# The seam between two layers, block by block: a trunk of one SSD layer and one dilated-attention layer, with the keys' matmul order, the adaLN dot products and GpSimd's residual moved

## The chip, the cores and the metric

The kernel runs on one core of a Trainium2 chip. The metric is the device time of one launch in microseconds. A core has engines that work side by side and wait for each other through semaphores: TensorE (PE in the profile; its weight loads are PEld), VectorE (DVE), ScalarE (ACT), GpSimd (POOL), and SyncE (SP), whose queue issues all DMA transfers of this kernel in program order.

## What is computed

256 tokens of width 2048 pass through two layers. Each layer computes x <- LayerNorm(alpha*x + (1+gate)*mixer(x*(1+scale)+shift)), where shift, scale and gate come from a second input c (adaLN). Cut to what matters here:

```python
def _adaln(c, w, b):
    mod = silu(c) @ w + b
    shift, scale, gate = split(mod, 3, axis=-1)
...
def reference(x, c, ada_w, ada_b, ln_g, ln_b, ..., a_out_w, kv_w, b_in_w, b_out_w):
    for layer in range(2):
        shift, scale, gate = _adaln(c, ada_w[layer], ada_b[layer])
        h = x * (1.0 + scale) + shift
        if layer == 0:
            y = _ssd_mixer(h, ..., a_out_w)        # y @ a_out_w at its end
        else:
            y = _dilated_mixer(h, k_sh, v_sh, b_in_w, b_out_w)
        x = _layer_norm(alpha * x + (1.0 + gate) * y, ln_g[layer], ln_b[layer])
        if layer == 0:
            k_sh, v_sh = _shared_kv(x, kv_w)       # split(x @ kv_w, 2), 3 groups x 8 heads x 128
    return x
```

The shared keys and values use the normalised x itself; the queries use h of the second layer. All arithmetic is float32.

## The kernel before

**Products.** A float32 matrix product is made of three products of rounded parts: weight high by activation high, low by high, and high by low. Each weight piece (512 KB, [128, 1024]) is loaded to `raw`; ScalarE rounds it to `whi` (L93) and VectorE subtracts to get `wlo` (L95). There are six `raw` buffers and four of `whi` and `wlo`, so loads run some pieces ahead of TensorE. Three forms of the product occur:

- `tm_chunk` / `tm_mults` (L172 to L174): tokens on the partitions of the result, 512 weight columns streamed; for each k-tile and each of the two blocks of 128 tokens three matmuls of 512 columns. With `split_end`, the last pieces of the chunk are held and run for block 0 first and then for block 1.
- `cm_piece` / `cm_quads` (L119 to L121): weight columns on the partitions, 256 tokens streamed; three matmuls of 256 columns for each k-tile and block of 128 weight columns.
- `cm_wide` (L151, L152): the same layout, but the activations' high and low parts lie side by side in `xp`, so one matmul of 512 columns covers high by both parts (L151) and one of 256 columns adds low by high (L152). For each k-tile the order is: 512 and 256 for the first block of columns, then 512 and 256 for the second. The eviction adds the two halves (L156 ScalarE, L157 VectorE).

**Order.** The kernel is written as one program; each engine runs its instructions in the order in which they were written, unless `issue_after` pins an instruction behind another. The order of the work around the change is this. Layer 0: projections and the scan, with the eight groups g of the scan; the output product `wout`, four chunks n of 512 columns with 32 k-tiles each. After chunk n, `residual` adds the gated result to x (L650, L651, on VectorE) and takes statistics (L652). Then `ln_scale` makes mean and reciprocal deviation for both blocks together with small operations (L659 to L664), and `u` is normalised, block 0 on ScalarE (L687) and block 1 on VectorE (L689). The function `x_tiles` transposes `u` in 128x128 tiles on TensorE (L702) and applies the norm's gain and offset per partition: `xhi` by ScalarE (L705), `xtmp` and `xlo` by VectorE (L706, L707). The tiles are made two k-tiles ahead of the products that use them.

The first products of layer 1 are the keys of the first half of the heads (`hq` 0), all three groups at once in six PSUM tiles with `cm_quads`; then the keys of the second half with `cm_wide` and all values with `tm_chunk`. After that x is scaled and shifted in place to h (L750, L196). `queries(0)` then runs 24 pieces of `wbin` through `cm_wide`, three groups of two column halves of four pieces each; the attention of those heads follows it, then the same for the second half, the gate and the output product. The attention bias `bs` (L766) is loaded at the start of the queries.

**adaLN dot products.** The modulation of a layer is 48 columns of 128 outputs. Each is one load of 1 MB (`araw`, L230) and one VectorE operation with accumulation (`dot`, L237). They are put in a list of jobs, and `background(n, every)` is called once after each weight piece: it adds n to a counter, and each time the counter reaches `every` one job is done. `queue` prepares them: two loads are always out. `pin` holds a VectorE instruction before which no dot may be placed. Rates before: 1 in 3 in the output chunks n = 1 to 3 (16 columns queued), 4 in 9 in the keys of `hq` 1 and the values (32 columns, 72 pieces). The counter also runs on while no job waits.

**GpSimd.** Once the transposes have read `u`, it is multiplied by the norm's gain row and its offset row is added (L759, L760), because the last residual needs x in this form. GpSimd does it for each quarter n of 512 columns and both blocks. The rows are broadcast loads of 256 KB (`lnr`, L63), in two tiles with two buffers each.

Of the kernel before, what the change touches and what calls it, by code (L numbers as in the profile page):

```python
# [9 lines left out]
F32 = mybir.dt.float32  # L10
# [39 lines left out]
def trunk(ctx, tc, xT, x, c, par, cst, bias, lnrow, ada, wdt, win, wout, wkv, wk1, wbin, wbout, out):  # L50
# [39 lines left out]
    def split(raw, into=None, after=None):  # L90

        hi, lo = into or [wp.tile([P, 1024], F32R, name=n, bufs=4) for n in ("whi", "wlo")]
        S.activation(hi, raw, AF.Copy)  # L93
        with tc.issue_after(after) if after is not None else ExitStack():
            latest[0] = V.tensor_tensor(lo, raw, hi.bitcast(F32), op=ALU.subtract)  # L95
        return hi.rearrange("p (k n) -> p k n", k=2), lo.rearrange("p (k n) -> p k n", k=2)

    jobs, latest, pin = [], [None], [None]

    def background(n, every=1):  # L100

        state[0] += n
# [19 lines left out]

    def cm_quads(work, ahi, alo, pre=None, after=None):
        for q in range(KT // 2):
            if pre:
                pre(q)
            for src, ps in work:
                cm_piece(src, q, ps, ahi, alo, after=after if q == 0 else None)
# [11 lines left out]
    def cm_wide(src, dst, rate=(0, 1)):  # L140
# [3 lines left out]
        for q in range(KT // 4):  # L144
            hi, lo = (t.rearrange("p k n -> p (k n)").rearrange("p (k n) -> p k n", k=4)
                      for t in split(load_piece(src[q])))
            for k in range(4):
                kt = 4 * q + k
                for n in range(2):
                    c_ = slice(n * P, n * P + P)  # L150
                    T.matmul(ps[n], hi[:, k, c_], xp[:, kt], start=kt == 0, stop=False, skip_group_check=True)  # L151
                    T.matmul(ps[n][:, 0, :], lo[:, k, c_], xhi[:, kt, :], start=False, stop=kt == KT - 1,  # L152
# [46 lines left out]
    sm.tile([P, 8], F32, name="pad", bufs=1)  # L199
# [72 lines left out]

    with ExitStack() as cA:
        pa = cA.enter_context(tc.tile_pool(name="pa", bufs=1))

        y = [pa.tile([P, 2, 512], F32, name=f"y{g}") for g in range(G)]
# [11 lines left out]
        with ExitStack() as cS:  # L288
# [305 lines left out]
            for g in range(G - 1):  # L594
                if g == 1:
                    pin[0] = latest[0].ins
# [57 lines left out]
        def ln_scale(blocks=(0, 1)):  # L654
# [3 lines left out]
            for i, b in enumerate(blocks):  # L658
# [9 lines left out]
                [(1, "gate", kt) for kt in range(KT)]  # L668
        for n in range(4):
            ps = tm_chunk(wout[n], lambda kt: yhi[kt // 16][:, kt % 16, :], lambda kt: ylo[kt // 4][:, kt % 4, :],  # L670
                          nk=2 * KT, rate=(1, 3) if n else (0, 1), pre=None if n else y_ahead,
                          split_end=2 if n == 3 else 0)
            if n == 0:
                queue(pn, cols1[:16])
# [6 lines left out]
        drain()  # L681
        r, nb, nb_last = ln_scale()
        for c0_, c1_ in ((0, 256), (256, 512), (512, 1024), (1024, 1536), (1536, 2048)):
            for b in range(2):
                cs_ = slice(c0_, c1_)
                if b == 0:
                    S.activation(u[b][:, cs_], u[b][:, cs_], AF.Identity, bias=nb[:, b:b + 1], scale=r[:, b:b + 1])  # L687
                else:
                    V.tensor_scalar(u[b][:, cs_], u[b][:, cs_], r[:, b:b + 1], nb[:, b:b + 1],  # L689
                                    op0=ALU.mult, op1=ALU.add)  # L690
# [7 lines left out]
    def x_tiles(q):  # L698
        for kt in (2 * q, 2 * q + 1):
            pt = aux.tile([P, 512], F32, name="aux")[:, :L]  # L700
            for b in range(2):
                T.transpose(pt[:, b * P:b * P + P], u[b][:, kt * P:kt * P + P], ident)  # L702
            t = pl.tile([P, L], F32, name="xtmp")
            g_, b_ = pv("lng")[:, kt:kt + 1], pv("lnb")[:, kt:kt + 1]
            S.activation(xhi[:, kt, :], pt, AF.Identity, bias=b_, scale=g_)  # L705
            V.tensor_scalar(t, pt, g_, b_, op0=ALU.mult, op1=ALU.add)  # L706
            V.tensor_tensor(xlo[:, kt, :], t, xhi[:, kt, :].bitcast(F32), op=ALU.subtract)  # L707

    def ahead(q):

        if q == 0:
            x_tiles(0)
        if q < KT // 2 - 1:
            x_tiles(q + 1)

    kk = [pb.tile([P, 12, L], F32, name=f"kk{i}").rearrange("p (g i) l -> p g i l", g=NG) for i in range(2)]
    vt = [pb.tile([P, NG, 2, 512], F32, name=f"vt{i}") for i in range(2)]

    def evict_k(hq, g, ps):
        for w in range(2):  # L720
            S.activation(kk[hq][:, g, 2 * w:2 * w + 2, :], ps[w], AF.Copy)

    with ExitStack() as cL:
        pl = cL.enter_context(tc.tile_pool(name="pl", bufs=3))
        ex = cL.enter_context(tc.tile_pool(name="ex1", bufs=2, space=PSUM))
        ps = [acc_pair(), acc_pair(), acc_pair(ex)]
        cm_quads([(wkv[2 * g], ps[g]) for g in range(NG)], xhi, xlo, pre=ahead, after=nb_last.ins)
        for g in range(NG):
            evict_k(0, g, ps[g])

        R = (4, 9)
        pin[0] = latest[0].ins
        with tc.issue_after(nb_last.ins):
            queue(pl, cols1[16:])
            jobs.append(lambda: gate_out(1))
            for g in range(NG):
                for w in range(2):
                    cm_wide(wk1[2 * g + w], kk[1][:, g, 2 * w:2 * w + 2, :], rate=R)
            for hq in range(2):
                for g in range(NG):  # L740
                    ps = tm_chunk(wkv[6 + 2 * g + hq], hx, lx, rate=R)
                    for b in range(2):
                        S.activation(vt[hq][:, g, b, :], ps[b], AF.Copy)
            drain()

# [6 lines left out]

        for n in range(4):
# [206 lines left out]
```

## Time and profile before

| | us |
|---|---|
| median of 3 runs | 1300.86 |
| lowest and highest | 1299.53, 1302.91 |
| the profiled execution | 1303.79 |
| its span | 1302.0 |
| its mean granted TensorE clock | 0.988 of full speed |

The profile comes from one execution. A page of it gives, for the whole span, the busy time of each engine, the chain of work that ended last, and groups of instructions by source line. Other views used here are the timeline (start, duration, engine, line, operation, output and inputs; in brackets how long the engine was idle before it and what ended that), windows (busy time of each engine in a stretch, the granted clock, the DMA engines' busy share and GB/s), and the waits of an engine. Matmuls are pipelined, so the duration of one is longer than the distance to the next; prices of matmuls are read from start to start. A few per cent of the matmul records can be missing.

### The profile page before, as it was taken

The page shows a single profiled execution, that of the slowest core. Times are in us where ns is not written, and L with a number is a line of the kernel's source. Part 1 is how long each engine was busy: PE and PEld are TensorE (multiplying, and loading weights), DVE is VectorE, ACT ScalarE, POOL GpSimd, SP SyncE. Part 2 cuts the span into 40 slices and gives each one's busy share as a digit, 9 for nine tenths or more (in the row PEclk, how much of TensorE's full clock was granted, in tenths as well). Part 3 has the DMA queues.
Part 4 walks back from the last instruction along what each step waited for, and adds up shares of the span by engine and source line. Part 5 has one row for each costly group of instructions (what it writes and reads, how often), then busy time and mean ns, then how long its engine had stood idle before and what let it go on. Part 6 is the DMA issues. An engine that isn't in the chain of part 4 may idle for free.

```text
span 1302.0 us, 19326 instructions
## 1 busy us (share of the span) xinstructions
PE 1244.2 (96%) x7378; PEld 1096.7 (84%) x7378; DVE 1028.6 (79%) x1457; ACT 709.6 (55%) x1036; POOL 26.6 (2%) x20
## 2 busy tenths in 40 slices
PE   4999999999999999999999799999999999999995
PEld 3878988899898999878888699888887888888884
DVE  6689887899998778899775577988777757758677
ACT  3544457867587686864333444444435645444651
POOL 0000000000000000000000043000000000000000
PEclk9999999999999999999999899999999999999998
DMA  9999967696884556389977575999897864353561
GB/s 381 421 367 419 382 205 249 221 345 243 288 312 152 187 180 209 117 324 331 383 262 218 190 244 163 354 376 367 329 344 268 274 192 146 106 189 95 162 259 65
DMA packets 80445, 335.86 MB, mean 258 GB/s; under 512 B 8960, under 2 KB 9056, under 8 KB 67552
## 3 DMA queue, kind: packets, MB, share of 16 engines
q1 hardware_dynamic: 80352, 334.62, 71.7%
q8 instruction: 58, 0.95, 0.3%
q14 instruction: 35, 0.29, 0.1%
HBM read 332.41 MB, written 2.18 MB: 257 GB/s over the span
## 4 chain that ended last, share of the span: by engine, by line
PE 82%; DVE 9%; DMA 4%; ACT 3%; issue 2%; SPq 0%; DVEq 0%; ACTq 0%
PE acc L151 13%; PE acc L173 12%; PE acc L174 11%; PE acc L172 11%; PE acc L121 8%; PE acc L120 8%; PE acc L119 8%; PE acc L152 6%; DMA araw<-in_ada 4%; DVE araw L237 2%; DVE wlo L95 2%; PE py L579 1%; PE aux L788 1%; ACT whi L93 1%; DVE cacc L306 1%
## 5 line engine op out<-in xcount | busy, mean ns | idle before, releaser
L95 DVE TENSOR_TENSOR wlo<-raw,whi 128x1024 fp32r<-128x1024 f32 x395 | 484.9, 1240 | 191.4 <-ACT whi L93 189.9
L93 ACT ACTIVATE whi<-raw 128x1024 fp32r<-128x1024 f32 x395 | 412.8, 1056 | 334.8 <-PE acc L174 140.8
L119 PE MATMUL acc<-actT,whi 128*128 128x256 f32 x960 | 274.1, 288 | 23.4 <-ACT whi L93 19.3
L173 PE MATMUL acc<-wlo,actT 128*128 128x512 f32 x704 | 277.2, 394 | 3.2 <-DVE wlo L95 3.1
L121 PE MATMUL acc<-actT,wlo 128*128 128x256 f32 x960 | 272.3, 288 | 4.5 <-DVE wlo L95 4.4
L120 PE MATMUL acc<-actT,whi 128*128 128x256 f32 x960 | 273.8, 286 | 0.6 <-DVE actT L384 0.6
L172 PE MATMUL acc<-whi,actT 128*128 128x512 f32 x704 | 272.9, 395 | 0.8 <-ACT actT L634 0.7
L151 PE MATMUL acc<-actT,whi 128*128 128x512 f32 x704 | 250.9, 398 | 0.0
L237 DVE SCALAR_TENSOR_TENSOR araw<-araw,cb__72 128x2048 f32<-128x2048 f32 x96 | 219.4, 2286 | 17.0 <-DMA araw<-in_ada 16.5
L119 PEld LDWEIGHTS acc<-actT,whi 128*128 128x128 f32 x960 | 186.8, 196 | 25.3 <-ACT whi L93 20.4
L152 PE MATMUL acc<-actT,wlo 128*128 128x256 f32 x704 | 201.4, 286 | 0.0
L121 PEld LDWEIGHTS acc<-actT,wlo 128*128 128x128 f32 x960 | 185.9, 195 | 7.1 <-DVE wlo L95 7.0
L120 PEld LDWEIGHTS acc<-actT,whi 128*128 128x128 f32 x960 | 187.7, 196 | 1.0 <-DVE actT L384 0.8
L174 PE MATMUL acc<-whi,actT 128*128 128x512 f32 x448 | 175.5, 392 | 0.0
L173 PEld LDWEIGHTS acc<-wlo,actT 128*128 128x128 f32 x704 | 132.7, 188 | 33.4 <-DVE wlo L95 6.9
L151 PEld LDWEIGHTS acc<-actT,whi 128*128 128x128 f32 x704 | 132.3, 188 | 30.2
L172 PEld LDWEIGHTS acc<-whi,actT 128*128 128x128 f32 x704 | 132.2, 188 | 28.7 <-ACT actT L634 1.5
L152 PEld LDWEIGHTS acc<-actT,wlo 128*128 128x128 f32 x704 | 133.2, 189 | 0.5
L174 PE MATMUL acc<-whi,ylo 128*128 128x512 f32 x256 | 100.3, 393 | 0.0
L174 PEld LDWEIGHTS acc<-whi,actT 128*128 128x128 f32 x448 | 84.4, 188 | 17.2
L174 PEld LDWEIGHTS acc<-whi,ylo 128*128 128x128 f32 x256 | 48.0, 188 | 9.7
L306 DVE SCALAR_TENSOR_TENSOR cacc<-acc,prm,cacc 128x253 f32<-128x253 f32 (+2 forms) x96 | 42.0, 474 | 6.6 <-ACT cacc L303 6.4
(204 smaller groups left out, 1077.8 us busy)
## 6 DMA issues: line engine op xcount, KB each, us to landing
araw<-in_ada SPq DMA_DIRECT2D x96, 1024.0 KB, 7.4
raw<-in_win SPq DMA_DIRECT2D x160, 512.0 KB, 5.4
raw<-in_wkv SPq DMA_DIRECT2D x72, 512.0 KB, 6.1
raw<-in_wout SPq DMA_DIRECT2D x64, 512.0 KB, 5.2
raw<-in_wbin SPq DMA_DIRECT2D x64, 512.0 KB, 3.6
raw<-in_wk SPq DMA_DIRECT2D x24, 512.0 KB, 7.8
cbc<-cumd SPq DMA_DIRECT2D x16, 512.0 KB, 5.2
raw<-in_wbout SPq DMA_DIRECT2D x16, 512.0 KB, 3.7
```

The lines of the kernel that those rows point to most:

```text
L93: S.activation(hi, raw, AF.Copy)
L95: latest[0] = V.tensor_tensor(lo, raw, hi.bitcast(F32), op=ALU.subtract)
L119: T.matmul(o, hi[:, k, c_], ahi[:, kt, :], start=first, stop=False, skip_group_check=True)
L120: T.matmul(o, hi[:, k, c_], alo[:, kt, :], start=False, stop=False, skip_group_check=True)
L121: T.matmul(o, lo[:, k, c_], ahi[:, kt, :], start=False, stop=kt == k1 - 1, skip_group_check=True)
L151: T.matmul(ps[n], hi[:, k, c_], xp[:, kt], start=kt == 0, stop=False, skip_group_check=True)
L152: T.matmul(ps[n][:, 0, :], lo[:, k, c_], xhi[:, kt, :], start=False, stop=kt == KT - 1, skip_group_check=True)
L172: T.matmul(ps[b], h_, hi[:, k, :], start=kt == k0, stop=False)
L173: T.matmul(ps[b], h_, lo[:, k, :], start=False, stop=False)
L174: T.matmul(ps[b], l_, hi[:, k, :], start=False, stop=kt == k1 - 1)
L237: V.scalar_tensor_tensor(raw, raw, 1.0, cb_, op0=ALU.mult, op1=ALU.mult, accum_out=mod[layer][:, ct, j:j + 1])
L306: V.scalar_tensor_tensor(acc[:, o:], ps[:, :L - o], w[:, j:j + 1], acc[:, o:], op0=ALU.mult, op1=ALU.add)
```

## The change

1. **The matmul order of `cm_wide`.** For each k-tile the two 512-column matmuls come first, then the two 256-column ones. Two PSUM tiles are now written in turn.
2. **All keys through `cm_wide`.** `cm_quads` and `x_tiles(q)` with its driver `ahead` are gone. The key weights are laid out on the host as pieces of 4 k-tiles by 256 columns. The first products of layer 1 are now the values of `hq` 0, groups 0 and 1 together, in `tm` form; then the values of group 2, then all keys (12 halves of 4 pieces), then the values of `hq` 1.
3. **The seam by token block.** The last output chunk is run with `split_end=4`: its last four pieces for block 0, then 24 matmuls for block 1. `residual`, `ln_scale` and the normalisation are written per block; of each block the first 512 columns are normalised at once. During this chunk the first four value pieces are loaded and split into buffers of their own (`first_v`, in the pool `slots`). The first four k-tiles are transposed and evicted for block 0 alone, then multiplied with these pieces, and then the same is done for block 1.
4. **Dots.** `background` sets its counter to zero while no job waits. Rates are 1 in 4 in the output chunks (11 columns, with `pin` at the third-last split of chunk 0) and 1 in 2 in the keys and values (37 columns, 80 pieces).
5. **GpSimd's residual** is written under `queries(0)`, behind the last weight split of the keys and values. Both rows of a quarter lie in the one buffer of `pT`, which the attention uses later. On the SP queue, the loads stand behind the bias and between weight pieces of `wbin`.
6. **Memory.** `y`, the first value pieces, the values and keys, the gated output and spare weight pieces share the tiles s0 to s7 and b8 to b11.

```diff
 def background(n, every=1):
-        state[0] += n
+        state[0] += n if jobs else -state[0]
         while state[0] >= every and jobs:
...
             for k in range(4):
                 kt = 4 * q + k
                 for n in range(2):
-                    c_ = slice(n * P, n * P + P)
-                    T.matmul(ps[n], hi[:, k, c_], xp[:, kt], start=kt == 0, stop=False, skip_group_check=True)
-                    T.matmul(ps[n][:, 0, :], lo[:, k, c_], xhi[:, kt, :], start=False, stop=kt == KT - 1,
+                    T.matmul(ps[n], hi[:, k, n * P:n * P + P], xp[:, kt], start=kt == 0, stop=False,
+                             skip_group_check=True)
+                for n in range(2):
+                    T.matmul(ps[n][:, 0, :], lo[:, k, n * P:n * P + P], xhi[:, kt, :], start=False, stop=kt == KT - 1,
                              skip_group_check=True)
...
+        def first_weights(q):
+
+            if q % 3 == 2 and q < 12:
+                i = q // 3
+                into = [slots.tile([P, 1024], F32R, name=f"s{2 * i + j}") for j in range(2)]
+                first_v.append(split(load_piece(wv[2 * (i % 2)][i // 2]), into=into))
+
         for n in range(4):
             ps = tm_chunk(wout[n], lambda kt: yhi[kt // 16][:, kt % 16, :], lambda kt: ylo[kt // 4][:, kt % 4, :],
-                          nk=2 * KT, rate=(1, 3) if n else (0, 1), pre=None if n else y_ahead,
-                          split_end=2 if n == 3 else 0)
+                          nk=2 * KT, rate=(1, 4) if n else (0, 1),
+                          pre={0: y_ahead, 3: first_weights}.get(n), split_end=4 if n == 3 else 0)
             if n == 0:
-                queue(pn, cols1[:16])
+                pin[0] = latest[-3].ins
+                queue(pn, cols1[:11])
+            if n == 3:
+                drain()
...
                 residual(n, ps[b], b, (gt, u[b][:, 512 * n:512 * n + 512]), xr)
-        drain()
-        r, nb, nb_last = ln_scale()
-        for c0_, c1_ in ((0, 256), (256, 512), (512, 1024), (1024, 1536), (1536, 2048)):
...
+                if n == 3:
+                    norm.append(ln_scale((b,)))
+                    normalise(b, 0, 256)
+                    normalise(b, 256, 512)
...
-        ex = cL.enter_context(tc.tile_pool(name="ex1", bufs=2, space=PSUM))
-        ps = [acc_pair(), acc_pair(), acc_pair(ex)]
-        cm_quads([(wkv[2 * g], ps[g]) for g in range(NG)], xhi, xlo, pre=ahead, after=nb_last.ins)
...
-        R = (4, 9)
-        pin[0] = latest[0].ins
+        vps = [tm_pair(), tm_pair()]
+        for b in range(2):
+            for kt in range(4):
+                tile4 = x_tile(kt, (b,))
+            for n in range(1, 4):
+                normalise(b, 512 * n, 512 * n + 512)
+            for i, w in enumerate(first_v):
+                if b and i == 2:
+                    x_tile(4)
+                    x_tile(5)
+                tm_mults(i // 2, w, vps[i % 2], hx, lx, 0, KT, (b,))
+        for q in range(2, KT // 2):
+            if q < KT // 2 - 1:
+                x_tile(2 * q + 2)
+                x_tile(2 * q + 3)
+            for j in range(2):
+                w = split(load_piece(wv[2 * j][q]), after=tile4.ins if q == 2 else None)
+                tm_mults(q, w, vps[j], hx, lx, 0, KT, range(2))
...
+        R = (1, 2)
+        pin[0] = latest[-1].ins
+        with tc.issue_after(tile4.ins):
+            queue(pl, cols1[11:])
             jobs.append(lambda: gate_out(1))
...
+            evict_v(0, 2, tm_chunk(wv[4], hx, lx, rate=R))
             for hq in range(2):
                 for g in range(NG):
...
+                    kv[hq, g] = place(3 + 3 * hq + g, [P, 4, L])
+                    for w in range(2):
+                        cm_wide(wk[2 * (2 * g + hq) + w], kv[hq, g][:, 2 * w:2 * w + 2, :], rate=R)
+            for g in range(NG):
+                evict_v(1, g, tm_chunk(wv[1 + 2 * g], hx, lx, rate=R))
             drain()
+            late = latest[-1].ins
...
-        for n in range(4):
-            cs_ = slice(512 * n, 512 * n + 512)
-            lnr = [pl.tile([P, 512], F32, name=f"lnr{i}", bufs=2) for i in range(2)]
...
+    for n in range(4):
+        cs_ = slice(512 * n, 512 * n + 512)
+        lnr = pc2.tile([P, NG, 384], F32, name="pT", bufs=1).rearrange("p g n -> p (g n)")
+        lnr = [lnr[:, 512 * i:512 * i + 512] for i in range(2)]
+        for i in range(2):
+            bcast(lnr[i], lnrow, i * D + 512 * n)
+        for b in range(2):
+            with tc.issue_after(late):
+                PO.tensor_tensor(u[b][:, cs_], u[b][:, cs_], lnr[0], op=ALU.mult)
+                PO.tensor_tensor(u[b][:, cs_], u[b][:, cs_], lnr[1], op=ALU.add)
```

113 lines of the change are left out of this document (45 added, 68 removed).

## The prediction

> **What bounds the kernel now.** I read the page first, for the engine that the end hangs on.
>
> ```profile
> PE 1244.2 (96%) x7378; PEld 1096.7 (84%) x7378; DVE 1028.6 (79%) x1457; ACT 709.6 (55%) x1036; POOL 26.6 (2%) x20
> ...
> PE 82%; DVE 9%; DMA 4%; ACT 3%; issue 2%; SPq 0%; DVEq 0%; ACTq 0%
> ```
>
> TensorE is busy for 96% of the span and carries 82% of the chain of waits. So the change can gain in three ways only: less idle on TensorE, less time at a reduced clock, or cheaper matmuls. The span is 1302.0 us and the profiled execution 1303.79 us; the median of the runs, 1300.86, lies 2.9 us below the latter, and the sum below is brought to the median with that.
>
> Then the windows around the seam between the layers (columns: busy time of PE, PEld, DVE, ACT, POOL, then the granted clock and the DMA share):
>
> ```profile
> 736.00:740.00 4.00, 0.79 (x4) 0.33 (x2) 3.45 (x10) 1.58 (x2) 0.00 (x0) 1.00 0.22 33
> 740.00:744.00 4.00, 1.33 (x4) 0.58 (x4) 3.69 (x15) 2.13 (x4) 0.00 (x0) 0.68 0.95 387
> 744.00:748.00 4.00, 2.46 (x12) 2.42 (x12) 3.70 (x8) 2.29 (x5) 0.00 (x0) 0.50 0.83 285
> 748.00:752.00 4.00, 4.00 (x22) 4.00 (x22) 3.71 (x6) 0.72 (x2) 0.09 (x1) 0.54 0.86 246
> ```
>
> In the first three TensorE is idle for 3.21 + 2.67 + 1.54 = 7.4 us. What it does run goes at a clock of 0.68, 0.50 and 0.54, which loses 0.32 x 1.33 + 0.50 x 2.46 + 0.46 x 4.00 = 3.5 us more. The seam costs 10.9 us. The timeline says why:
>
> ```profile
> 736.17 0.39 PE L173 MATMUL acc<-wlo,actT 128*128 128x512 f32 x1
> ...
> 736.40 0.39 PE L174 MATMUL acc<-whi,ylo 128*128 128x512 f32 x1
> ...
> 736.83 0.69 DVE L650 TENSOR_TENSOR u<-acc,gt 128x512 f32<-128x512 f32 x1 [0.28 <-PE acc L174]
> ...
> 741.67 0.16 DVE L664 SCALAR_TENSOR_TENSOR m01nb<-m01mv,m01y 128x2 f32<-128x2 f32 x1
> ...
> 741.87 3.21 ACT L687 ACTIVATE u<-u,m01nb,m01y 128x256 f32<-128x256 f32 x5 [3.99 <-DVE m01nb L664]
> ...
> 742.52 1.52 PE L702 MATMUL aux<-cc,u 128*128 128x128 f32 x4 [5.73 <-ACT u L687]
> ...
> 745.58 1.65 PE L119 MATMUL acc<-actT,whi 128*128 128x256 f32 x6 [1.54 <-ACT actT L705]
> ```
>
> From the last output matmul of layer 0 everything hangs on VectorE: the residual and statistics of token block 1, then small steps, 741.83 - 736.83 = 5.0 us in all, before the first normalised column and its transpose.
>
> Two smaller losses stand in the waits of TensorE between 300 and 600 us, and the timeline shows both behind VectorE's adaLN dots (L237), which sat waiting for their weights:
>
> ```profile
> PE aux L632 <- DVE ylo L635: 1.0, 1, 1.0
> ...
> 389.67 2.29 DVE L237 SCALAR_TENSOR_TENSOR araw<-araw,cb__72 128x2048 f32<-128x2048 f32 x1 [2.05 <-DMA araw<-in_ada]
> ...
> 393.06 0.96 PE L549 MATMUL aux<-cc,xs 128*128 128x128 f32 x4 [2.00 <-ACT cb L528]
> ...
> 396.38 0.54 PE L172 MATMUL acc<-whi,actT 128*128 128x512 f32 x1
> ```
>
> **The change part by part.** *The seam.* The last four pieces of the output chunk are now run for block 0 first, then 24 matmuls for block 1. At 0.23 us from L173 to L174 these last 5.4 us, and they cover block 0's chain of 5.0 us. I lay out what follows from VectorE's start on block 0 as zero. ScalarE normalises block 0 at 5.1; by 742.52 - 741.87 its transposes start 0.65 us later, and with four of them and an eviction the first V product comes at about 6.8 (745.58 - 742.52 = 3.1 us at half clock for both blocks, here one block), where block 1's matmuls ended at 5.2: 1.6 us, 0.4 of it transposes that are work anyhow. The first low half needs VectorE, which is at block 1's three residual steps (three like L650, 2.2 us from 5.4 to 7.6) and then makes xtmp and xlo: 1.3 us of wait, to 8.95. Block 0's 24 products run to about 13.8, while block 1's chain, 5.0 us plus the xtmp and xlo steps interleaved with it, ends near 12.8; its normalise, transpose and eviction leave 0.7 us more, and 0.3 us is lost at two later low halves. That is 3.4 us of idle in place of 7.4.
>
> The clock is the second half of it. At 393 the 2.0 us wait was followed by matmuls at half rate until 396.4. Three waits of 1.6, 1.3 and 0.7 us within 9 us lie close to that; I charge one such stretch of 3.4 us at half speed, 1.7 us. The bounds are none and two. The seam then costs 5.1 (3.4 to 6.8) where it cost 10.9: **-5.8** (-7.5 to -4.1). The ScalarE norms, the split pieces and their loads were there before; only their place changes. Four k-tiles are transposed and evicted per block, in halves; that is in the schedule.
>
> The Trainium skill, "TensorE: Matmul & The Clock Gate", Part 1, has the clock halve only after an idle window of about 3.4 us. By that rule the new seam would stay at full speed and the sum be 1.7 us lower, 3.4 with the stretch charged under the queries. The trace speaks against it: 2.0 us of wait, ended by four transposes, was enough at 393.
>
> *Keys through the wide form, in a new order.* The price of each form is the distance between starts:
>
> ```profile
> 770.20 0.28 PE L119 MATMUL acc<-actT,whi 128*128 128x256 f32 x1
> 770.32 0.28 PE L120 MATMUL acc<-actT,whi 128*128 128x256 f32 x1
> ...
> 860.06 0.40 PE L151 MATMUL acc<-actT,whi 128*128 128x512 f32 x1
> 860.30 0.28 PE L152 MATMUL acc<-actT,wlo 128*128 128x256 f32 x1
> ...
> 861.12 0.40 PE L151 MATMUL acc<-actT,whi 128*128 128x512 f32 x1
> ...
> 1139.83 0.39 PE L151 MATMUL acc<-actT,whi 128*128 128x512 f32 x1
> ...
> 1140.87 0.39 PE L151 MATMUL acc<-actT,whi 128*128 128x512 f32 x1
> ```
>
> Three 256-column matmuls take 0.36 us. Three wide pairs lie between each two of the last four rows: 1.06 us at 860, 0.353 a pair, and 1.04 us at 1140, 0.347. The keys of the first half have 12 column blocks x 16 k-tiles = 192 units. What distinguishes 860 from 1140 the trace doesn't tell. If it is the alternation of sizes, the new order (512, 512, 256, 256) halves the changes and takes half of the 0.0067 us that 1.06 and 1.04 differ by in a pair: 192 x (0.360 - 0.350) = **-1.9**, bounds -2.6 and 0. For the 704 pairs (L151 x704) that exist already, half of it is 704 x 0.0033 = **-2.3**. The bounds are all of it, -4.7, and, should it be the change of accumulator, which now comes twice as often, +4.7.
>
> *Dots counted evenly.* The counter no longer saves up while no job waits, so the dots that ran close together up to 392 are spread out. In the new order the step that TensorE waited for (cb) stands ahead of the dot on VectorE, and the dot's load is issued long before. The 2.0 us and 3.4 us at half speed go (-3.7). In the output phase the first dot now stands after the tiles that L632 needs: -1.0. Together **-4.7**, bound 0 if the wait moves elsewhere. Under the keys and values a dot now comes with every second piece, where it was four in nine:
>
> ```profile
> 820.00:840.00 20.00, 20.00 (x117) 17.41 (x116) 18.17 (x18) 9.03 (x11) 0.00 (x0) 1.00 0.92 351
> 840.00:860.00 20.00, 20.00 (x115) 17.33 (x114) 18.60 (x20) 8.53 (x11) 0.00 (x0) 1.00 1.02 413
> ...
> L95 DVE TENSOR_TENSOR wlo<-raw,whi 128x1024 fp32r<-128x1024 f32 x24 | 28.9, 1222 | 5.0 <-ACT whi L93 5.0
> L237 DVE SCALAR_TENSOR_TENSOR araw<-araw,cb__72 128x2048 f32<-128x2048 f32 x12 | 27.4, 2286 | 3.1 <-DMA araw<-in_ada 3.1
> L157 DVE TENSOR_TENSOR kk<-acc,kk 128x256 f32<-128x256 f32 x10 | 4.0, 420 | 0.9 <-ACT kk L156 0.9
> ```
>
> The groups are those of 822 to 886 us. Four key pieces need 4 x 1.22 + 2 x 2.29 + 2 x 0.42 = 10.3 us of VectorE, against 32 pairs = 11.2 us of TensorE; their 4 MB (2 of weights, 2 for the dots) in 11.2 us are 375 GB/s, and the row at 840 moved 413. TensorE's matmuls hide both, with 8 and 9% to spare: 0. If DMA gave no more than the 351 GB/s of the row at 820, the 37 dots and 80 pieces (80.7 MB) would take 230 us, 6 us over TensorE's 224.
>
> *GpSimd's residual under the queries.* Here I find a cost. Both norm rows of each quarter now lie in one buffer, so the SP queue stops at the next quarter's load until GpSimd is done with the last, and the weight loads of the queries stand behind it. The queue reads: eight query pieces, the bias, rows 0, pieces 9 and 10, rows 1, 11 and 12, rows 2, 13 and 14, rows 3, 15 and 16, then free.
>
> ```profile
> 1020.71 0.39 PE L151 MATMUL acc<-actT,whi 128*128 128x512 f32 x1
> ...
> 1024.85 0.33 SPq L766 DMA_DIRECT2D bs<-in_bias  x1
> ...
> 1030.16 0.49 DVE L790 SCALAR_TENSOR_TENSOR bi<-bs 128x128 f32<-128x128 f32 x2 [1.41 <-DMA bs<-in_bias]
> ...
> 767.15 3.52 POOL L759 TENSOR_TENSOR u<-u,lnr 128x512 f32<-128x512 f32 x2 [8.04 <-issue]
> 770.64 2.91 POOL L760 TENSOR_TENSOR u<-u,lnr 128x512 f32<-128x512 f32 x2
> 785.29 3.54 POOL L759 TENSOR_TENSOR u<-u,lnr 128x512 f32<-128x512 f32 x2 [11.74 <-issue]
> ...
> L93 ACT ACTIVATE whi<-raw 128x1024 fp32r<-128x1024 f32 x395 | 412.8, 1056 | 334.8 <-PE acc L174 140.8
> ...
> raw<-in_wbin SPq DMA_DIRECT2D x64, 512.0 KB, 3.6
> lnr<-in_lnrow SPq DMA_DIRECT2D x8, 256.0 KB, 5.4
> out<-u SPq DMA_DIRECT2D x8, 256.0 KB, 2.5
> ```
>
> On the old clock the queries begin at 1020.7, and a piece (8 pairs) takes 2.8 us, so piece 15 is due at 1060. The bias goes out at 1024.85 and lands at 1030; rows 0 right behind, and GpSimd's 6.45 us end at 1037.3. Rows 1 and 2 each cost a landing and 6.45: with 3.2 us for two loads on an almost empty queue (between 2.5 and 5.4) rows 3 go out at 1057, piece 15 behind them, landing 3.6 and two split steps of 1.1 (L93) and 1.2 us (L95) later, at about 1063. **+3.0** of wait on piece 15, and **+1.7** for the stretch at half speed. Bounds: 0 (landings of 2.5, less than 2 us late, a clock that holds) and +12.6 (landings of 5.4 from rows 0 on, two stretches).
>
> The sum: -5.8 - 1.9 - 2.3 - 4.7 + 4.7 = **-10.0**, so 1293.8 for the profiled execution and **1291** for the median.
>
> **The rivals.** *The queue of norm rows decides (slower).* At the old place GpSimd waited 8.0 and 11.7 us between rounds. If a round under the queries takes 11.7 + 6.45 as well, rows 3 go out at 1037 + 2 x 18.2 = 1073.6 and piece 15 is ready at 1079.5: 19.5 us late, with two stretches of half clock +23 in place of +4.7, and 1309. It turns the sum positive from a wait of some 7.5 us a round. For it: those two rows, and the queue order. Against it: those waits came from loads held up by weight pieces whose buffers TensorE had not released, and here the two pieces between the rows take buffers released long before.
>
> *The seam keeps its length.* The wait for block 1 takes the place of the one for block 0, and half clock covers it all: without the -5.8, 1297. For it: VectorE is busy 3.7 of each 4 us there, and gets the same work. Against: 5.4 us of matmuls now lie beside the chain.
>
> *The new matmul order costs.* +4.7 for -2.3 and 0 for -1.9: 1300, no change. For it: two neighbouring 256-column matmuls as in L119 to L121 take 0.12 each, 0.36 for three, no better than the pair. Against: 512 after 512 takes 0.23 at 736 and 256 after 256 0.12 at 770, which add up to the cheap pair at 1140.
>
> *Nothing waits under the queries, and the clock holds at both places:* -16.4, 1284.5.
>
> **How the numbers follow.** The forecast has 0.50, the slower rival 0.13, the unchanged seam 0.13, the costly order 0.11, the smooth case 0.13. What a measurement of this kernel can tell from no change is about 0.3%, 3.9 us. Faster by more are the forecast, the smooth case and most of the unchanged seam, 0.75; the costly order and the rest of the seam are the same, 0.12; slower 0.13. The range goes from all lower bounds without a queue wait (-7.5 - 2.6 - 4.7 - 4.7 = -19.5, 1281; I take 1280) to just past the costly order, 1301; beyond it lies the slower rival alone. The forecast's own range is 1285 to 1297.
>
> **What would show it.** Right: one wait of TensorE of 1 to 2 us before the first V product and one for xlo, with clock above 0.5 in most of the seam; no wait at L549's and L632's successors; wide pairs 0.347 to 0.350 apart throughout; a wait of TensorE for a query's whi or wlo some 40 us into the queries, behind a weight load issued after GpSimd's third round. Wrong: pairs at 0.36, GpSimd rounds more than 14 us apart, waits for wlo behind dots under the keys, or a seam with over 7 us of idle.

## The result and the profile after

The changed kernel takes 1309.29 us (median of 5 runs, 1307.16 to 1313.01), the kernel before 1300.34 us beside it (1297.91 to 1302.91). The ratio is 1.0073 with a 95% interval of 1.0055 to 1.0092: it became slower by 9 us, where 1291 was forecast.

The profiled execution after has a span of 1305.4 us and took 1307.16 us. That is the quickest of its five runs, while the profiled one of before was 3.5 us above its median, so the two profiles differ by 3.4 us only. Much of this spread lies in the first 104 us: at the same matmul there, the eleven profiles taken here stand between 101.3 and 107.0 us, before anything that the change touches. The comparison therefore goes by stages within an execution. The lines of this table are worked out from start times of matmuls in the timelines: the stage begins with the first named matmul and ends with the next (us).

| stage | before | after | difference |
|---|---|---|---|
| that matmul to the last output matmul of layer 0 (scan, output product) | 632.1 | 636.0 | +3.9 |
| to the first query matmul (seam, keys, values) | 284.3 | 276.0 | -8.3 |
| to the first score (24 query pieces) | 67.8 | 74.2 | +6.4 |
| to the last wide matmul (attention, second queries, gate) | 153.4 | 153.4 | 0.0 |
| to the last matmul (output product of layer 1) | 43.9 | 45.7 | +1.9 |

So what was to be gained at the seam was gained, and it was given back three times. The stages add up to 3.9 us of loss, while the medians differ by 9; in which stage the other 5 us lie, these two executions don't show. The waits of TensorE in the changed kernel show where. The view gives the line that waited, what released it, total us, times, and the longest; first from 200 to 600 us, then from 1015 to 1095, then from 700 to 800:

```profile
PE aux L546 <- ACT cb L525: 3.9, 3, 2.8
PE py L576 <- DVE xd L548: 2.0, 1, 2.0
...
PE acc L146 <- DVE wlo L95: 2.8, 2, 1.4
PE acc L143 <- ACT whi L93: 2.1, 1, 2.1
...
PE acc L166 <- ACT actT L715: 0.9, 2, 0.4
PE aux L712 <- ACT u L671: 0.3, 1, 0.3
PE aux L712 <- DVE xtmp L716: 0.2, 1, 0.2
```

L546 and L576 are in the scan (L549 and L579 before). The wait of 2.0 us that began at 391 has gone, but there are waits of 2.8 and 2.0 us at other places. The last three lines are the seam: 1.4 us in all, where one wait of 5.7 us stood. The windows of the changed kernel at those places:

```profile
300.00:310.00 10.00, 7.41 (x41) 6.05 (x40) 10.00 (x21) 3.81 (x8) 0.00 (x0) 0.84 0.53 219
390.00:400.00 10.00, 10.00 (x54) 8.61 (x54) 9.71 (x17) 5.38 (x8) 0.00 (x0) 1.00 0.90 313
530.00:540.00 10.00, 7.24 (x36) 6.02 (x34) 8.04 (x19) 8.71 (x20) 0.00 (x0) 0.77 0.06 7
...
736.00:740.00 4.00, 4.00 (x19) 3.20 (x18) 3.32 (x16) 3.16 (x4) 0.00 (x0) 1.00 0.01 5
740.00:744.00 4.00, 2.98 (x12) 1.59 (x11) 3.57 (x12) 4.00 (x9) 0.00 (x0) 1.00 0.28 63
744.00:748.00 4.00, 4.00 (x20) 3.25 (x19) 3.76 (x17) 1.49 (x3) 0.00 (x0) 1.00 1.01 424
748.00:752.00 4.00, 3.56 (x18) 2.68 (x17) 3.08 (x11) 1.62 (x4) 0.00 (x0) 1.00 0.09 37
...
1050.00:1060.00 10.00, 6.15 (x33) 4.86 (x32) 3.62 (x3) 2.50 (x3) 5.28 (x5) 1.00 0.82 254
1060.00:1070.00 10.00, 8.97 (x43) 7.88 (x44) 7.40 (x8) 5.33 (x9) 0.00 (x0) 0.83 0.94 351
```

At the seam TensorE is idle for 1.5 us in 16, and the clock stays at 1.00. At 300, 530 and 1050 it is idle for 2.6, 2.8 and 3.9 us in 10, and a clock of 0.77 to 0.84 follows.

The queries' loss is read off the SP queue (start of the first issue and the span of those in the row, x of them) and GpSimd:

```profile
1017.90 0.90 SPq L63 DMA_DIRECT2D pT<-in_lnrow  x2
1019.38 1.46 SPq L87 DMA_DIRECT2D raw<-in_wbin  x2
1031.07 0.81 SPq L63 DMA_DIRECT2D pT<-in_lnrow  x2
1031.97 0.85 SPq L87 DMA_DIRECT2D raw<-in_wbin  x2
1040.74 0.81 SPq L63 DMA_DIRECT2D pT<-in_lnrow  x2
...
1050.34 0.81 SPq L63 DMA_DIRECT2D pT<-in_lnrow  x2
1051.23 38.72 SPq L87 DMA_DIRECT2D raw<-in_wbin  x19
...
1024.01 2.55 POOL L793 TENSOR_TENSOR u<-u,pT 128x512 f32<-128x512 f32 x2 [1023.57 <-DVE wlo L95]
1026.51 4.53 POOL L794 TENSOR_TENSOR u<-u,pT 128x512 f32<-128x512 f32 x2
1035.66 2.55 POOL L793 TENSOR_TENSOR u<-u,pT 128x512 f32<-128x512 f32 x2 [4.62 <-PE acc L146]
1038.17 2.55 POOL L794 TENSOR_TENSOR u<-u,pT 128x512 f32<-128x512 f32 x2
```

Each pair of row loads is issued when GpSimd has ended the round before (1031.07 after 1031.04, 1040.74 after 1040.72). Two weight pieces follow each of them, in place of a steady stream. A round takes 9.6 us, and in it TensorE is given 5.6 us of work.

### The profile page after: what moved, and what is told of

The parts are those of the page before. It is cut to its first block, busy times and chain, and to the rows that moved or that the text cites. A ratio compares the mean times of both kernels' runs of the same rounds, so it can differ in the third digit from the quotient of the medians.

```text
span 1305.4 us, 19008 instructions
## 1 busy us (share of the span) xinstructions
PE 1244.3 (95%) x7186; PEld 1083.3 (83%) x7186; DVE 1029.4 (79%) x1490; ACT 702.3 (54%) x1040; POOL 22.3 (2%) x20
## 4 chain that ended last, share of the span: by engine, by line
PE 80%; DVE 9%; ACT 4%; DMA 4%; issue 3%; SPq 0%; DVEq 0%; ACTq 0%
PE acc L143 13%; PE acc L167 12%; PE acc L168 12%; PE acc L166 12%; PE acc L146 7%; PE acc L121 6%; PE acc L120 6%; PE acc L119 6%; DVE wlo L95 3%; DMA araw<-in_ada 3%; DVE araw L231 3%; PE py L576 2%; ACT whi L93 2%; PE aux L813 1%; DVE cacc L303 1%
## 5 line engine op out<-in xcount | busy, mean ns | idle before, releaser
L95 DVE TENSOR_TENSOR wlo<-raw,whi 128x1024 fp32r<-128x1024 f32 x391 | 477.3, 1233 | 181.4 <-ACT whi L93 169.6
L143 PE MATMUL acc<-actT,whi 128*128 128x512 f32 x896 | 287.1, 399 | 2.1 <-ACT whi L93 2.1
L167 PE MATMUL acc<-wlo,actT 128*128 128x512 f32 x688 | 271.6, 395 | 2.7 <-DVE wlo L95 2.6
L166 PE MATMUL acc<-whi,actT 128*128 128x512 f32 x688 | 267.0, 394 | 0.5 <-ACT actT L631 0.5
L119 PE MATMUL acc<-actT,whi 128*128 128x256 f32 x768 | 219.1, 288 | 21.9 <-ACT whi L93 19.2
L121 PE MATMUL acc<-actT,wlo 128*128 128x256 f32 x768 | 217.2, 288 | 3.4 <-DVE wlo L95 3.3
L120 PE MATMUL acc<-actT,whi 128*128 128x256 f32 x768 | 218.8, 286 | 0.6 <-DVE actT L381 0.6
L146 PEld LDWEIGHTS acc<-actT,wlo 128*128 128x128 f32 x896 | 167.9, 189 | 45.1 <-DVE wlo L95 7.9
L146 PE MATMUL acc<-actT,wlo 128*128 128x256 f32 x896 | 182.7, 284 | 4.5 <-DVE wlo L95 3.7
L168 PE MATMUL acc<-whi,actT 128*128 128x512 f32 x432 | 169.3, 392 | 0.0
L119 PEld LDWEIGHTS acc<-actT,whi 128*128 128x128 f32 x768 | 149.2, 195 | 24.0 <-ACT whi L93 20.3
L120 PEld LDWEIGHTS acc<-actT,whi 128*128 128x128 f32 x768 | 150.1, 195 | 1.2 <-DVE actT L381 0.8
L166 PEld LDWEIGHTS acc<-whi,actT 128*128 128x128 f32 x688 | 128.9, 188 | 26.5 <-ACT actT L631 1.1
L143 PEld LDWEIGHTS acc<-actT,whi 128*128 128x128 f32 x896 | 138.3, 190 | 2.6 <-ACT whi L93 2.3
L168 PEld LDWEIGHTS acc<-whi,actT 128*128 128x128 f32 x432 | 81.4, 188 | 17.1 <-issue 0.5
L535 ACT ACTIVATE seg<-cbc,cumT 128x128 f32<-128x128 f32 x128 | 40.7, 388 | 13.4 <-PE py L576 12.7
```

Of the source, the lines that this page charges most:

```text
L95: latest.append(V.tensor_tensor(lo, raw, hi.bitcast(F32), op=ALU.subtract))
L119: T.matmul(o, hi[:, k, c_], ahi[:, kt, :], start=first, stop=False, skip_group_check=True)
L120: T.matmul(o, hi[:, k, c_], alo[:, kt, :], start=False, stop=False, skip_group_check=True)
L121: T.matmul(o, lo[:, k, c_], ahi[:, kt, :], start=False, stop=kt == k1 - 1, skip_group_check=True)
L143: T.matmul(ps[n], hi[:, k, n * P:n * P + P], xp[:, kt], start=kt == 0, stop=False, skip_group_check=True)
L146: T.matmul(ps[n][:, 0, :], lo[:, k, n * P:n * P + P], xhi[:, kt, :], start=False, stop=kt == KT - 1, skip_group_check=True)
```

## The experiments

Each was timed in five rounds beside the kernel before, with a profile. The theory after the result: the 9 us are two separate losses, the queue of norm rows under the queries, and the counter set to zero, which moves the dots in the scan and with them the order in which the other engines do the scan's steps.

**rows_free.** The changed kernel, with room for the rows in a buffer that the queries don't use yet:

```diff
-        lnr = pc2.tile([P, NG, 384], F32, name="pT", bufs=1).rearrange("p g n -> p (g n)")
-        lnr = [lnr[:, 512 * i:512 * i + 512] for i in range(2)]
+        if n == 0:
+            rows = pc2.tile([P, 12, L], F32, name="qq").rearrange("p g n -> p (g n)")
+        if n == 3:
+            rows = pc2.tile([P, NG, 384], F32, name="pT", bufs=1).rearrange("p g n -> p (g n)")
+        lnr = [rows[:, 1024 * (n % 3) + 512 * i:1024 * (n % 3) + 512 * i + 512] for i in range(2)]
```

> The changed kernel, with the norm rows of the first three quarters in a buffer that the queries do not use yet, and those of the last in pT: no load on the SP queue waits for GpSimd any more. Theory (the queue): the first queries took 74.2 us in the changed kernel and 67.7 in the one before, and the new matmul spacing of 0.3483 a pair makes 192 x 0.3483 = 66.9 of them; so the waits at 1049 to 1059 go, the stage comes to 67 us, and the time falls by 7 us from 1309 to about 1302. Rival (GpSimd beside the queries' weight splits slows VectorE, wherever the rows lie): the waits stay, 1309.

Measured: 1301.13 us (ratio to before 1.0001, 0.9987 to 1.0015), 8.2 us less than the changed kernel. The query stage takes 66.87 us in its timeline, and TensorE waits for nothing in it. The queue and GpSimd:

```profile
1016.43 4.26 SPq L63 DMA_DIRECT2D qq<-in_lnrow  x6
1020.74 2.43 SPq L63 DMA_DIRECT2D pT<-in_lnrow  x2
1023.26 24.52 SPq L87 DMA_DIRECT2D raw<-in_wbin  x13
...
1039.61 4.50 POOL L797 TENSOR_TENSOR u<-u,qq 128x512 f32<-128x512 f32 x2
...
1032.51 8.22 DVE L95 TENSOR_TENSOR wlo<-raw,whi 128x1024 fp32r<-128x1024 f32 x4 [3.81 <-ACT whi L93]
```

All rows are issued in one go, and the pieces flow. GpSimd now runs against VectorE's splits without a pause and both are slowed: two of its operations take 4.50 us (2.55 in the changed kernel's second round), and four splits 8.22 us, 2.06 each. No time is lost by it, since the splits run ahead of TensorE. The rival, contention as the cause, falls; the queue is the cause.

**scan_counter.** The changed kernel, with the counter running through the scan as it did before:

```diff
-        state[0] += n if jobs else -state[0]
+        state[0] += n if jobs or not even else -state[0]
...
         first_v, norm = [], []
+        even.append(True)
+        state[0] = 0
```

> The changed kernel, with the counter of the dots left running through layer 0's scan as before, and set to zero only from the output product on. Theory (the reset reorders the scan): ScalarE's order in the scan is that of the kernel before again, so the waits at 302 and 532 go and the one at 390 comes back; by the two profiles the scan ends 3.5 us earlier, by the medians up to 9: 1301 to 1306. Rival (the scan's new waits come from the shared tiles that y now lies in): they stay, and the wait at 390 is added, 1309 to 1313.

Measured: 1300.73 us (0.9994, 0.9980 to 1.0009), 8.6 us less than the changed kernel. From 104 us to the last output matmul it takes 629.1 us, against 636.0. The waits of TensorE from 200 to 600 us:

```profile
PE aux L546 <- ACT cb L525: 2.1, 2, 1.8
```

The wait of 2.8 us and that for xd have gone, and the one before L546 is back: 1.8 us, until 395. `y` lies in the shared tiles here too, so these are not the cause.

**rows_and_counter.** Both edits.

> Both edits at once. Theory: the losses are separate and add up, -7 and -3.5 or more from 1309: 1293 to 1298, 2 to 7 us faster than the kernel before, which is the seam and the keys (8.3 us by the profiles) less what the last stage loses (1.8). Rival (something else in keys and values or in memory costs the 9 us): no faster than the kernel before, 1300 to 1309.

Measured: 1292.80 us (0.9942, 0.9924 to 0.9960). That is 16.5 us less than the changed kernel; 8.2 and 8.6 add up to 16.8. The two losses are separate, and together they are more than the whole 9 us. These are differences of medians whose ratios are good to about 2 us each; by the stages of the profiles the two losses are 7.3 us (74.18 to 66.87, the queries) and 6.9 (636.0 to 629.1, the scan and output product).

**before_reset.** The kernel before with one line changed:

```diff
-        state[0] += n
+        state[0] += n if jobs else -state[0]
```

> The kernel before, with nothing changed but the counter of the dots, which is set to zero while no job waits. Theory (the reset reorders the scan): the waits of the changed kernel at 302 and 532 appear, the one at 390 goes, and the time rises by 3 to 8 us, to 1303 to 1308. Rival (the prediction's reasoning: the reset only takes the dots away from cb): 1295 to 1297.

Measured: 1313.75 us (1.0093, 1.0073 to 1.0114), 12.5 us slower. The waits from 200 to 600 us:

```profile
PE aux L549 <- ACT cb L528: 3.6, 2, 2.8
PE py L579 <- DVE xd L551: 2.0, 1, 2.0
PE aux L632 <- DVE ylo L635: 1.5, 2, 1.1
```

These are the two waits of the changed kernel, and a third one: this kernel keeps the old rate of one dot in three in the output chunks, and its dots get in front of the tiles there at 585 and 599. The size was above the expected 3 to 8 us, partly by that: following the same matmul in both timelines, the scan after 104 us loses 4.3 us and the start of the output product 2.7, 7.0 in all; a further 2.7 came before 104 us, where ScalarE and VectorE run the same instructions in the same order in both kernels, which is spread and not effect. The rest of the 12.5 is not placed. What the one line does is told by ScalarE's timeline at the same step, first before, then in the changed kernel:

```profile
530.33 0.59 ACT L582 ACTIVATE py<-y 128x512 f32<-128x512 f32 x1
...
531.56 0.26 ACT L528 ACTIVATE cb<-aux 128x128 f32<-128x128 f32 x1
```

```profile
531.07 1.28 ACT L537 ACT_TABLE_LOAD   x1
532.36 1.06 ACT L537 ACTIVATE seg<-seg 128x1024 f32<-128x1024 f32 x1
533.33 0.58 ACT L579 ACTIVATE py<-s 128x512 f32<-128x512 f32 x1
...
534.55 0.25 ACT L525 ACTIVATE cb<-aux 128x128 f32<-128x128 f32 x1
```

In the changed kernel a table load and an exponential of 128x1024 stand ahead of the two squares (L579; L582 before) and of `cb`, 2.3 us in all, and TensorE starts L546 at 534.86 when `cb` is there. No dot stands in the 100 us ahead of this place (the last one starts at 419.2). It is the order of ScalarE's instructions that is another one: the two programs part at 258 to 260 us, just behind the first dot of the scan in the kernel before (254.0), and stay apart until its end. scan_counter and rows_and_counter, where the counter runs, have ScalarE's order of before throughout the scan, and before_reset has that of the changed kernel. TensorE's order goes with it: behind a run of projections that starts at 257 us in both, the next transposes L549 start at 260.4 in the kernel before, and L546, which is the same line, at 297.6 in the changed one. So, other than the description of the kernel says, an engine's order is not the written one. The program asks for a dot after every fifth piece of the scan, and in the changed kernel's trace 1 to 8 splits lie between one dot and the next. What places the instructions isn't shown here; rows_free has the changed kernel's order instruction by instruction on ScalarE and VectorE, so it belongs to the program and not to the execution.

**scan_rate6** and **scan_rate4.** rows_free with the dots of the scan at other rates:

```diff
-            R = (1, 5)
+            R = (1, 6)
```

> The version with the norm rows in their own buffer and the counter set to zero as in the changed kernel (1301.1 us), with a dot after every sixth piece of the scan instead of every fifth. Theory (any other place of the dots gives ScalarE and VectorE another order in the scan, and with it other waits of TensorE): the waits at 302 and 532 move, go or are joined by others, anywhere from 1292 to 1306, and ScalarE's order differs from both. Rival (a counter set to zero costs because dots ran together before): as with every fifth, 1300 to 1302, waits in the same steps.

> As scan_rate6, with a dot after every fourth piece of the scan. Theory: again other waits, anywhere from 1292 to 1306. Rival: denser dots load VectorE more beside the scan's own work, and the time rises above 1302 in order of the rate (sixth below fifth below fourth).

Measured: 1301.67 us (1.0002, 0.9991 to 1.0013) for every sixth piece, 1295.05 us (0.9947, 0.9936 to 0.9959) for every fourth, beside 1301.13 for every fifth. The scan and output stage takes 636.4, 631.7 and 637.1 us. Every sixth has the waits of every fifth because it moved nothing in the scan: ScalarE runs the same order in both traces, VectorE too but for one small copy at 542 us, and each of the 16 dots stands behind the same split. This run repeats rows_free and tests neither its theory nor its rival. Every fourth moved one dot against the splits, the sixth. Here are the fifth and the sixth, first in rows_free, then in scan_rate4:

```profile
285.56 2.28 DVE L231 SCALAR_TENSOR_TENSOR araw<-araw,cb__72 128x2048 f32<-128x2048 f32 x1
...
294.27 2.29 DVE L231 SCALAR_TENSOR_TENSOR araw<-araw,cb__72 128x2048 f32<-128x2048 f32 x1
```

```profile
288.85 2.29 DVE L231 SCALAR_TENSOR_TENSOR araw<-araw,cb__72 128x2048 f32<-128x2048 f32 x1
...
292.20 2.29 DVE L231 SCALAR_TENSOR_TENSOR araw<-araw,cb__72 128x2048 f32<-128x2048 f32 x1
```

Three splits lie between them in rows_free and one in scan_rate4. This is the first place where VectorE's order differs. ScalarE's differs from 301 us on, in 14 places until the end of the scan, and TensorE's waits are others:

```profile
PE acc L119 <- DVE cacc L303: 2.0, 1, 2.0
...
PE py L576 <- DVE xd L548: 0.7, 1, 0.7
```

One dot, two splits earlier, goes with 5.4 us less in the stage and 6 by the medians. The dots are no denser over the scan, so the rival of scan_rate4, the load of VectorE, isn't tested either; what a place of the dots brings can't be read from the rate.

**old_order.** rows_and_counter with the old order of the wide matmuls:

```diff
                 for n in range(2):
                     T.matmul(ps[n], hi[:, k, n * P:n * P + P], xp[:, kt], ...)
-                for n in range(2):
                     T.matmul(ps[n][:, 0, :], lo[:, k, n * P:n * P + P], xhi[:, kt, :], ...)
```

> The version with both edits (norm rows in their own buffer, counter running through the scan; 1292.8 us), with cm_wide's matmuls in the old order 512, 256, 512, 256. Theory (the new order is worth 0.005 us a pair in most stages): 384 pairs of keys and 192 of the first queries at 0.3533 again, 576 x 0.005 = 2.9 us more, the second queries 0.3 less; and if the last stage's new wait of 1.3 us at the first output weights comes from the two evictions that now fall together, it goes, -1.8: 1293 to 1296, with pairs 0.3533 apart in the profile. Rival (two accumulators written in turn cost): 1290 to 1292.

Measured: 1293.31 us (0.9938, 0.9926 to 0.9950), against 1292.80: no difference that five rounds can tell. By stages the two halves of the theory are there. The seam with the keys and values takes 0.4 us more, the first queries 1.0 more, the stage from the first score to the last wide matmul 1.2 more (88.55 and 65.72 against 87.84 and 65.24), and the last stage 1.9 less (43.90 against 45.75).

**seam_two.** rows_and_counter with two pieces, and not four, held for block 1:

```diff
-                          pre={0: y_ahead, 3: first_weights}.get(n), split_end=4 if n == 3 else 0)
+                          pre={0: y_ahead, 3: first_weights}.get(n), split_end=2 if n == 3 else 0)
```

> The version with both edits, with split_end=2 for the last output chunk: 12 matmuls of block 1 (2.7 us) stand behind block 0's last ones, and not 24. Theory (these matmuls cover block 0's chain of 5.0 us on VectorE): 2.7 us more idle before the first value product, and 1.7 for a stretch at half clock if that brings one: 1295.5 to 1297.2. Rival (the idle of the seam is set by block 1's chain or by the split weights): 1292 to 1293.5.

Measured: 1299.40 us (0.9986, 0.9977 to 0.9996), 6.6 us more than rows_and_counter (5.9 by the stage of seam, keys and values), above the theory's 4.4. Its waits from 700 to 800 us and its windows:

```profile
PE aux L714 <- ACT u L673: 4.6, 1, 4.6
...
734.00:738.00 4.00, 0.62 (x2) 0.29 (x2) 3.75 (x25) 1.27 (x3) 0.00 (x0) 0.76 0.60 193
738.00:742.00 4.00, 3.15 (x9) 2.43 (x9) 3.98 (x13) 3.32 (x7) 0.00 (x0) 0.50 0.79 332
```

12 matmuls less beside VectorE's chain bring 4.3 us more wait (4.6 for 0.3), and half clock behind it. That the wait grew by more than 2.7 us is in VectorE's timeline: block 1's residual steps (from 733.04 on) now come among block 0's small steps, which end at 736.69, 6.6 us after they began and not 5.0.

**gate_old_order.** rows_and_counter with the old order of matmuls for the gate's products alone (`stagger`, a new argument, gives `cm_wide` that order):

```diff
-            cm_wide(wbin[2 * (6 + hq) + w], z)
+            cm_wide(wbin[2 * (6 + hq) + w], z, stagger=True)
```

> The version with both edits (1292.8 us), with the old matmul order only for the gate's products in the last wide stage, the new one for keys and queries. Theory (evictions that fall together delay the first output weights): the last stage comes from 45.75 back to 43.9 us, the gate's stage loses 0.5: 1291 to 1292, by the profile's last wait of 1.3 us gone. Rival (the last stage's wait comes from the spare tiles that the output weights now lie in): it stays, 1293 to 1294.

Measured: 1290.91 us (0.9912, 0.9897 to 0.9926). The last stage is back at 43.85 us, and no wait of TensorE is left after 1180 us. By its median it is the quickest version here: 10.9 us faster than the kernel before, 18 than the changed one.

## Why the prediction was wrong

**The step that failed** is "Dots counted evenly: together **-4.7**, bound 0 if the wait moves elsewhere". The two waits that it named did go: between the matmuls around 387 and 416 us the changed kernel gains 4.2 us on the one before, and around 571 us 1.6. But the same edit gave TensorE two new waits, of 2.0 us at 302 and 2.8 us at 532. Followed matmul by matmul these cost 4.0 us (from 283 to 322) and 6.2 us (from 516 to 543) with the half clock behind them. The undone edit is worth 8.6 us, the edit alone costs 12.5. The step looked at the places where a dot had stood in the way, and took the order of all else as given. It isn't: where the dots stand elsewhere, ScalarE and TensorE have another order too, until the end of the scan, and in scan_rate4 a single moved dot was enough. The bound "0 if the wait moves" was one wait for one wait, and the loss was outside the range because of it.

**GpSimd under the queries, +4.7.** The place, the queue order and the rhythm were as worked out: stops behind the rows, 35 to 45 us into the queries, with rounds 9.6 us apart as in the sum (3.2 and 6.45). That the rounds agree is luck, since GpSimd waited 4.6 us for the first of two rows and its four operations took 5.05. The wait was mis-sized: the loss is 7.3 us by the stage (74.18 and 66.87) and 8.2 by the medians. Two terms were too small. From the issue of piece 15 (1051.23) to the start of its rounding on ScalarE (1057.82) it took 6.6 us, where the sum has 3.6 for the landing; and its split on VectorE, beside GpSimd, took 2.07 and not 1.2. Piece 13 had the same, 6.6 and 2.09, so already its low half came late (1.4 us at 1051), then piece 15 (2.1 us) and its low half (1.4). The slowed splits are a part of the two low halves' waits, some 0.9 us of each; in rows_free they are as slow and nothing waits. The bound of +12.6 held it.

**The slower rival** had 1309 us, and 1309 was measured, but not by its mechanism: the rounds were 9.6 us apart and not 18. The number agrees by accident.

**The seam, -5.8.** Seam, keys and values together gained 8.3 us. The keys' share by the matmul spacing is 192 x (0.360 - 0.348) + 192 x (0.353 - 0.348) = 3.3, and 3.3 were lost to the dots (below); so about 8 are the seam's, small gaps elsewhere in the stage included, which is past the bound of 7.5. (The idle terms of that step, 1.2, 1.3, 0.7 and 0.3, add up to 3.5 and not 3.4.) The waits that the schedule had are there but shorter (0.2 to 0.4 us each in place of 1.6, 1.3 and 0.7), and no stretch at half clock came. seam_two shows that the cover of block 0's chain is what the gain rests on: 2.7 us of cover are worth 6.6 by the medians.

**The matmul order, -2.3 and -1.9.** The spacing became even, as predicted, at 0.348 in place of the expected 0.350 and of 0.353 or 0.347 before:

```profile
837.82 0.63 PE L143 MATMUL acc<-actT,whi 128*128 128x512 f32 x2
838.29 0.39 PE L146 MATMUL acc<-actT,wlo 128*128 128x256 f32 x2
838.51 0.62 PE L143 MATMUL acc<-actT,whi 128*128 128x512 f32 x2
```

Two pairs are 0.69 us apart. The 2.6 us that the stages of old_order lose show the gain. It was given back at an unforeseen place: both accumulators of a wide half now end together, and early in the output product of layer 1, at 1251, the low part of a weight came 1.3 us late. The forecast had no term for this +1.9. That it is the order and not the shared tiles is shown by gate_old_order, which keeps the tiles; by which step the joint evictions delay that weight isn't shown.

**Dots under keys and values, 0.** Wrong by 3.3 us. From 884 us on, in the second half of the keys, TensorE stops for the low part of a weight once in every fourth piece. The timeline of the changed kernel, TensorE and then VectorE:

```profile
907.63 0.63 PE L143 MATMUL acc<-actT,whi 128*128 128x512 f32 x2
909.20 0.51 PE L146 MATMUL acc<-actT,wlo 128*128 128x256 f32 x2 [0.94 <-DVE wlo L95]
...
920.00 0.63 PE L143 MATMUL acc<-actT,whi 128*128 128x512 f32 x2
920.77 0.51 PE L146 MATMUL acc<-actT,wlo 128*128 128x256 f32 x2
```

```profile
905.32 2.28 DVE L231 SCALAR_TENSOR_TENSOR araw<-araw,cb__72 128x2048 f32<-128x2048 f32 x1
...
907.93 2.35 DVE L95 TENSOR_TENSOR wlo<-raw,whi 128x1024 fp32r<-128x1024 f32 x2
```

The split stands behind a dot. From the first L143 of a row to L146 it is 0.47 us without a wait (837.82 to 838.29 above), 0.77 at 920 and 1.57 at 907; with what follows them, six such stops add up to 3.3 us. The estimate compared VectorE's sum of work with TensorE's, 10.3 with 11.2 us, and took 8% to be enough; one dot of 2.3 us at the wrong moment is a fifth of that period.

**The clock.** The Trainium skill, "TensorE: Matmul & The Clock Gate", Part 1, asks for an idle window of about 3.4 us before the rate is halved. The trace again differs: a wait of 2.0 us at 302, with one of 0.4 before it, lies in a window at 0.84, and one of 2.8 us at 532 in a window at 0.77. At 1059 and 1061 two waits stand close together, 2.1 and 1.4 us, and the window from 1060 on is at 0.83. But the wait of 1.8 us in scan_counter left its window (390 to 400) at 1.00, and so did the short waits of the seam, 1.4 us in all within 9 us, where the prediction had charged 1.7 us; so far the rule was nearer than my step.

Put together by the stages, the kernel lost 3.9 us ahead of the seam in place of gaining 4.7, lost 6.4 under the queries in place of 4.1 (4.7 less the order's 0.6), lost 1.9 in the last stage where nothing was foreseen, and gained 8.3 in between. The forecast had 8.3 there too (5.8, 1.9 and 0.6), but its parts were others, and so that agreement is luck. The 1.0 that it had from the matmul order in the attention stage (second queries and gate) doesn't show, 153.4 before and after; old_order finds 1.2 there, so something else in that stage takes it back.

## What to carry to other kernels

Where the order of the instructions is not the written one, an edit that only moves background work can reorder the foreground: compare each engine's order far behind the edit, not just at the waits to be removed, and measure such an edit alone. Compare the orders also before calling an edit tested, since the trace can show that it moved nothing. A tile with one buffer that is filled by a shared DMA queue turns every use of it into a stop for all that is queued behind; count the pieces that stand behind each stop and the time at which they are due. When several edits come together, time the ones that can be undone in a line first: here two small parts of the change cost 16.5 us and hid a gain of 7.5 (1300.3 to 1292.8).

## What the hardware showed beside this

GpSimd's operations on the rows and VectorE's splits slow each other: 2.55 us for two of 128x512 while VectorE ran nothing (at 1035.66 in the changed kernel) and 4.50 beside splits, whose own time went from 1.22 to 2.06 us. The Trainium skill, "SBUF — State Buffer", section "SBUF: two separate sides", has an exclusive lock on a shared port pair for a VectorE operation with two SBUF inputs against a GpSimd operation that reads SBUF. The direction agrees. But a split and one such operation alone, 1.22 and 1.28 us, would take 2.50 in strict turn, and 2.06 and 2.25 were measured, so here they exclude each other for most of their length and not for all of it.

Why the old order of matmuls ran at 0.353 us a pair in most stages and at 0.347 in one stays open. The even 0.348 of the new order says only that the changes from one size to the other have a part in it.
